# Two layers of a conditioned token mixer on one core: modulation products and half of a depthwise convolution moved from VectorE to GpSimd and ScalarE

## The chip, the core and the metric

One core of a Trainium2 chip. PE is TensorE (PEld its weight loads), DVE is VectorE, ACT is ScalarE, POOL is GpSimd, and SP issues the DMAs. The metric is the device time of one execution in microseconds, the median of a few; less is faster.

## What is computed

Two blocks of two layers each, on 512 tokens of width 1024. The change touches the first block only. Cut to that:

```python
for l in range(2):
    mod = silu(c) @ w_ada[l] + b_ada[l]          # [1, 6*1024]: "modulation"
    sh1, sc1, g1, sh2, sc2, g2 = split(mod, 6)
    h = rmsnorm(x, norm1_w[l]) * (1 + sc1) + sh1
    x = x + g1 * token_mixers(h, ...)            # convolution, attention, recurrence
    h = rmsnorm(x, norm2_w[l]) * (1 + sc2) + sh2
    x = x + g2 * conv_ffn(h, ...)
# inside token_mixers: proj = h @ w_in, split into ten parts; then
a = a_val * sigmoid(a_gate)                      # 256 channels
a = depthwise_conv(a, conv_a_w, 31 taps) + conv_a_b
a = silu(layernorm(a))
# beside it: attention over 6 heads, and a gated recurrence over 6 heads
```

The second block (sparse attention, gated linear attention, feed-forward) follows and is the same in both kernels.

## The kernel before

Activations lie with channels on the 128 partitions and the 512 tokens along the row, in fp32. A matrix product is made three times on PE from two halves of each number: a high part H (rounded to the fast fp32 type) and the rest L. So each tile of weights comes by DMA into `wraw`, ACT copies it to `wH` (line 311) and POOL subtracts to give `wL` (line 312); PE can use a tile only after both. There are 4 `wraw` and 6 `wH`/`wL` buffers.

**Modulation.** `ada` (line 520) makes one column of `mod` (128 of the 6144 numbers) at a time: a DMA of 512 KB into the tile `ada`, one DVE instruction that multiplies it with the conditioning row `c` and sums each row into `mod[:, j]` (line 528, with a small instruction that reads the accumulator), and one DVE instruction that adds the bias to this column (line 531). Columns 0 to 15 of layer 0 are made in the opening with six buffers. All others have one buffer in all, so each DMA waits for the product before it. They are a generator, `work`; `step(n)` takes n of them, and is called once for each block of projected columns in a mixer (22 times, and 3 at its end) and in a feed-forward's first half (44 times). Of layer 0 the columns 16 to 39 fall into its mixer; 44 more fall into its feed-forward; the last 12 of layer 1 fall into layer 1's mixer. Then come 50 empty steps and the table of sines for block 2.

**The mixer.** `weave` interleaves generators by their costs: each advances by cost/n, and the one that stands lowest is next. `heads(0)` and `heads(1)` (n = 93, 95) are the recurrence and then attention; `fill` (n = 100 in layer 0, 115 in layer 1) the projections and other dense products; `conv` (n = 210) the convolution. In `conv`, `conv_taps` makes the two tiles one after the other: ACT makes the first tap (line 562), and DVE the other 30 with one instruction each (line 566), y = pad * w + y. Then `conv_norm` and `conv_silu`.

The recurrence works on three pairs of heads. Each has seven levels and a crossing: ACT copies operands (line 738) of K and Q, DVE multiplies Q by a decay (line 746, `rW`) and POOL multiplies K (line 747, `rK`), PE makes 32 small products (line 706), and DVE puts them into an accumulator under a mask (line 761). The eight K products of a pair mark where the recurrence stands: they run from 77 to 125, 157 to 207 and 207 to 251 us in layer 0, and from 814 to 847, 907 to 962 and 962 to 1001 us in layer 1. Below, these are pair 0, 1 and 2.

All engines run their instructions in the order in which the scheduler of the framework wrote them, each waiting for what it needs; SP issues DMAs in such an order too.

## Time and profile before

| | |
|---|---|
| median of 3 runs (lowest, highest) | 3408.36 us (3407.62, 3408.36) |
| the profiled execution | 3403.52 us, of it the span of its instructions 3401.7 us |
| mean granted clock of TensorE | 0.983 of full speed |
| busy over the span: PE, DVE, ACT, POOL | 96%, 52%, 47%, 51% |
| layer 0: opening and mixer, feed-forward | 0 to about 410, to about 790 us |
| layer 1's mixer | about 790 to 1160 us |

Shares over the whole span say little here, since each stage has its own limits; the rows below are cut to the stages that the change touches. A clock of 1.00 is 2.4 GHz and 0.50 is 1.2 GHz, so a stretch's mean lies between.

### The profile page before, as it was taken

The numbers are of one execution on the slowest core, as the hardware profiler recorded it, in microseconds if no ns is written. First come the engines' busy times: TensorE is split into PE (matmuls) and PEld (weight loads), VectorE is DVE, ScalarE is ACT, GpSimd is POOL, SyncE is SP. The second block draws the span as 40 slices with busy tenths as digits, with TensorE's granted clock in tenths as the row PEclk, the third lists the DMA queues.
The fourth block names the chain that finished last, engine by engine and source line by source line (L and its number), as shares of the span: only waits on it lengthen the run. The fifth ranks groups of instructions, "written<-read, shape, count | busy, mean of one in ns | idle before, by whom it ended". The sixth has DMA issues, their size and how long they took to land.

```text
span 3401.7 us, 46240 instructions
## 1 busy us (share of the span) xinstructions
PE 3263.0 (96%) x16546; PEld 2655.2 (78%) x16546; DVE 1777.1 (52%) x3029; ACT 1589.6 (47%) x3104; POOL 1744.5 (51%) x1442
## 2 busy tenths in 40 slices
PE   8799999998899999999999999999999999999998
PEld 6677787787766888887878777888878787778887
DVE  8987677607976633226740735332367407353332
ACT  4457543334466544435343645443353436454433
POOL 5542366555542455553445447565634454476654
PEclk9899999999899999999999999999999999999999
DMA  6323355542212322332213132333322131322232
GB/s 231 108 71 99 115 176 178 179 132 97 87 46 68 103 99 96 99 108 86 87 57 101 52 108 81 98 97 93 102 76 87 57 101 51 108 81 98 96 94 80
DMA packets 174445, 338.92 MB, mean 100 GB/s; under 512 B 20388, under 2 KB 27428, under 8 KB 174215
## 3 DMA queue, kind: packets, MB, share of 16 engines
q1 hardware_dynamic: 174214, 335.97, 31.1%
q8 instruction: 130, 2.13, 0.3%
q14 instruction: 101, 0.82, 0.1%
HBM read 325.28 MB, written 8.91 MB: 98 GB/s over the span
## 4 chain that ended last, share of the span: by engine, by line
PE 76%; DVE 11%; issue 4%; ACT 3%; POOL 3%; DMA 2%; SPq 0%; POOLq 0%; ACTq 0%; DVEq 0%
PE p L332 22%; PE p L333 21%; PE p L334 21%; POOL wL L312 2%; DVE cv L566 2%; PE s L706 2%; DVE ada L528 1%; DMA ada<-in_w_ada 1%; PE s L1424 1%; PE s L895 1%; PE t L867 1%; PE o L625 1%; PE o L626 1%; PE s L894 1%; DVE rW L746 1%
## 5 line engine op out<-in xcount | busy, mean ns | idle before, releaser
L312 POOL TENSOR_TENSOR wL<-wraw,wH 128x512 fp32r<-128x512 f32 x996 | 1334.6, 1348 | 1278.4 <-ACT wH L311 1184.3
L332 PE MATMUL p<-hH,wH 128*128 128x512 f32 (+1 forms) x2808 | 1080.9, 386 | 12.2 <-ACT hH L311 7.5
L333 PE MATMUL p<-hL,wH 128*128 128x512 f32 (+1 forms) x2808 | 1069.5, 381 | 12.7 <-POOL hL L312 10.2
L334 PE MATMUL p<-hH,wL 128*128 128x512 f32 (+1 forms) x2808 | 1065.5, 380 | 6.2 <-POOL wL L312 6.2
L311 ACT CAST wH<-wraw 128x512 fp32r<-128x512 f32 x996 | 607.0, 613 | 947.9 <-PE p L333 436.9
L332 PEld LDWEIGHTS p<-hH,wH 128*128 128x128 f32 x2808 | 536.4, 191 | 122.4 <-issue 14.0
L333 PEld LDWEIGHTS p<-hL,wH 128*128 128x128 f32 x2808 | 537.4, 191 | 111.1 <-POOL hL L312 12.2
L334 PEld LDWEIGHTS p<-hH,wL 128*128 128x128 f32 x2808 | 536.8, 191 | 107.2 <-POOL wL L312 10.0
L1142 DVE SCALAR_TENSOR_TENSOR y<-p,vec,y 128x511 f32<-128x511 f32 (+1 forms) x264 | 196.8, 748 | 484.9 <-ACT y L1139 297.4
L332 PE MATMUL p<-aH,wH 128*128 128x512 f32 (+1 forms) x704 | 266.5, 379 | 2.9 <-ACT aH L311 2.9
L333 PE MATMUL p<-aL,wH 128*128 128x512 f32 (+1 forms) x704 | 266.5, 379 | 0.6 <-POOL aL L312 0.6
L334 PE MATMUL p<-aH,wL 128*128 128x512 f32 (+1 forms) x704 | 265.6, 377 | 0.6 <-POOL wL L312 0.6
L332 PE MATMUL p<-wH,hH 128*128 128x256 f32 x704 | 202.4, 287 | 0.0
L333 PE MATMUL p<-wL,hH 128*128 128x256 f32 x704 | 201.4, 286 | 0.0
L334 PE MATMUL p<-wH,hL 128*128 128x256 f32 x704 | 200.3, 284 | 0.0
L528 DVE SCALAR_TENSOR_TENSOR ada<-ada,c 128x1024 f32<-128x1024 f32 x96 | 144.2, 1502 | 44.3 <-DMA ada<-in_w_ada 43.6
L312 POOL TENSOR_TENSOR aL<-y,aH 128x512 fp32r<-128x512 f32 x88 | 113.9, 1295 | 98.2 <-ACT aH L311 98.2
L332 PEld LDWEIGHTS p<-aH,wH 128*128 128x128 f32 x704 | 133.2, 189 | 27.7 <-ACT aH L311 3.4
L333 PEld LDWEIGHTS p<-aL,wH 128*128 128x128 f32 x704 | 133.1, 189 | 25.8 <-POOL aL L312 1.1
L334 PEld LDWEIGHTS p<-aH,wL 128*128 128x128 f32 x704 | 133.1, 189 | 25.5 <-POOL wL L312 1.0
L706 PE MATMUL s<-rS,rS 64*128 64x128 f32 (+1 forms) x864 | 111.6, 317 | 33.9 <-DVE rW L761 21.2
L332 PEld LDWEIGHTS p<-wH,hH 128*128 128x128 f32 x704 | 135.8, 193 | 3.7 <-issue 2.9
(338 smaller groups left out, 4736.9 us busy)
## 6 DMA issues: line engine op xcount, KB each, us to landing
ada<-in_w_ada SPq DMA_DIRECT2D x96, 512.0 KB
wraw<-in_w1up SPq DMA_DIRECT2D x176, 256.0 KB
wraw<-in_w2up SPq DMA_DIRECT2D x176, 256.0 KB
wraw<-in_w2cm SPq DMA_DIRECT2D x164, 256.0 KB
wraw<-in_w1dn SPq DMA_DIRECT2D x80, 256.0 KB
wraw<-in_w2dn SPq DMA_DIRECT2D x80, 256.0 KB
wraw<-in_w1cm SPq DMA_DIRECT2D x72, 256.0 KB
wraw<-in_w2tm SPq DMA_DIRECT2D x64, 256.0 KB
```

What stands on the lines that cost most here:

```text
L311: self.nc.scalar.copy(H, src)
L312: (eng or self.nc.vector).tensor_sub(L, src, H.bitcast(F32))
L332: self.product = first = mm(out, a[0], b[0], start=start, stop=False, **kw)
L333: mm(out, a[0], b[1], start=False, stop=False, **kw)
L334: mm(out, a[1], b[0], start=False, stop=stop, **kw)
L528: ins = nc.vector.scalar_tensor_tensor(w, w, 1.0, c, op0=OP.mult, op1=OP.mult, accum_out=mod[:, j:j + 1])
L566: nc.vector.scalar_tensor_tensor(y, pad[:, j:j + S], w, y, op0=OP.mult, op1=OP.add)
L625: nc.tensor.matmul(o, v[:, i], SH[:, i], start=i == 0, stop=False)
L626: nc.tensor.matmul(o, v[:, i], SL[:, i], start=False, stop=i == n - 1)
L706: N.nc.tensor.matmul(p[:, at:at + w], K[r, ks], Q[r, qs], start=True, stop=True)
L746: nc.vector.tensor_mul(view(Q), view(Q), pattern(t, 1, (b - 1, 2), (2, m), (0, n)))
L1142: nc.vector.scalar_tensor_tensor(y[:, -d:], p[:, :S + d], c[:, i:i + 1], y[:, -d:], op0=OP.mult, op1=OP.add)
```

## The change

1. In layer 0, the columns 16 to 39 (24 of them) are made with `split`: POOL multiplies the tile by `c` in place (line 535 of the changed kernel), and ACT copies it in place with a sum of each row (line 536). All other columns stay on DVE.
2. The bias is added for a group of columns at once (`add_bias`, line 522): 15 additions in place of 96.
3. In the feed-forward, `step(2)` is called for each of the seven blocks of the second half as well: 14 columns more are made there. So layer 1's mixer holds none, and the table of sines moves from layer 1's mixer to the end of layer 0's feed-forward.
4. The convolution's two tiles are two threads of `weave`, which begin at once (n = 105 and 60, each 30 taps). Tile 0 stays on DVE. For tile 1, ACT makes each tap's product into a single buffer `ct` (line 580) and POOL adds it (line 581). `conv_norm` follows when both are done.

```diff
-CONV = (0, 210)
+CONV = (105, 60)
...
-def ada(N, l, c, mod, vec, order, pool, bufs):
+def ada(N, l, c, mod, vec, groups, pool, bufs, split=False):
...
+    for g in groups:
+        for j in range(48)[g]:
+            yield
+            w = N.tile(pool, [128, D], "ada", bufs)
+            nc.sync.dma_start(w, N.I["w_ada"][l, j])
+            if split:
+                ins = nc.gpsimd.tensor_mul(w, w, c)
+                nc.scalar.activation(w, w, AF.Copy, accum_out=mod[:, j:j + 1])
+            else:
+                ins = nc.vector.scalar_tensor_tensor(w, w, 1.0, c, op0=OP.mult, op1=OP.mult, accum_out=mod[:, j:j + 1])
...
+        add_bias(N, mod, vec, g)
...
-        nc.vector.scalar_tensor_tensor(y, pad[:, j:j + S], w, y, op0=OP.mult, op1=OP.add)
+        if i == 0:
+            nc.vector.scalar_tensor_tensor(y, pad[:, j:j + S], w, y, op0=OP.mult, op1=OP.add)
+        else:
+            t = N.tile(P, [128, S], "ct", 1)
+            nc.scalar.activation(t, pad[:, j:j + S], AF.Copy, scale=w)
+            nc.gpsimd.tensor_add(y, y, t)
...
-        weave((heads(0), HEADS), (delay(heads(1), LAG, 1), HEADS + LAG), (fill, FILL[l]), (delay(conv(), CONV[0], 1), CONV[1]))
+        weave((heads(0), HEADS), (delay(heads(1), LAG, 1), HEADS + LAG), (fill, FILL[l]), (conv(), CONV[0]), (taps(1), CONV[1]))
...
-        work = itertools.chain(ada(N, 0, c, mods[0], vecs[0], range(16, 48), B, 1),
-                               ada(N, 1, c, mods[1], vecs[1], range(48), B, 1),
+        parts = slice(0, 16), slice(16, 24), slice(24, 40), slice(40, 48)
+        work = itertools.chain(ada(N, 0, c, mods[0], vecs[0], parts[1:3], B, 1, True),
+                               ada(N, 0, c, mods[0], vecs[0], parts[3:], B, 1),
+                               ada(N, 1, c, mods[1], vecs[1], parts, B, 1),
...
-            norm.take(ct, N.dense(dn[ct], a), FULL)
+            p = N.dense(dn[ct], a)
+            step(2)
+            norm.take(ct, p, FULL)
```

**POOL in layer 0, pair 0.** From the third K product (`rK` with the decay of 4 tokens) to the fourth there stood the subtractions for two tiles of weights, two small ones for attention values (`VJ`) and another tile; the fifth K product came right behind the fourth:

```order
L747 TENSOR_TENSOR rK_601<-rK_601,rT_147_744 128x2x64x4
L312 TENSOR_TENSOR wL_992<-wraw_989,wH_991 128x512
L312 TENSOR_TENSOR wL_998<-wraw_995,wH_997 128x512
L616 TENSOR_TENSOR VJ_1112<-V_733,VJ_1112 128x4x64
L616 TENSOR_TENSOR VJ_1115<-V_733,VJ_1115 128x4x64
L312 TENSOR_TENSOR wL_1099<-wraw_1096,wH_1098 128x512
L747 TENSOR_TENSOR rK_601<-rK_601,rT_148_746 128x2x32x8
L747 TENSOR_TENSOR rK_601<-rK_601,rT_149_748 128x2x16x16
```

In the changed kernel the same stretch holds two modulation products and four additions of tile 1 (`cv_807`) as well:

```order
L762 TENSOR_TENSOR rK_593<-rK_593,rT_147_736 128x2x64x4
L535 TENSOR_TENSOR ada_761<-ada_761,c 128x1024
L581 TENSOR_TENSOR cv_807<-cv_807,ct_929 128x512
L581 TENSOR_TENSOR cv_807<-cv_807,ct_946 128x512
L312 TENSOR_TENSOR wL_994<-wraw_991,wH_993 128x512
L312 TENSOR_TENSOR wL_1000<-wraw_997,wH_999 128x512
L581 TENSOR_TENSOR cv_807<-cv_807,ct_978 128x512
L535 TENSOR_TENSOR ada_765<-ada_765,c 128x1024
L312 TENSOR_TENSOR wL_1103<-wraw_1100,wH_1102 128x512
L581 TENSOR_TENSOR cv_807<-cv_807,ct_1023 128x512
L762 TENSOR_TENSOR rK_593<-rK_593,rT_148_738 128x2x32x8
```

Over pair 0, from its first K product to its last, 5 products and 14 additions come in; between pair 0 and pair 1, 3 and 5; in pair 1, 3 and 11; to the end of pair 2, 3 more products. DVE's 30 taps of tile 0 stand ahead of the end of pair 0, all but one; before, 30 of the 60 did.

**SP at the end of layer 0's mixer.** The last three modulation columns of the group stand among the loads of `x` and of the first weights of the feed-forward (`w1up`). Before, four loads of `x` stood behind each of the last two:

```order
L527 DMA ada_3404<-in_w_ada 128x1024
L297 DMA x_3415<-in_x 128x512
L297 DMA x_3416<-in_x 128x512
L297 DMA x_3417<-in_x 128x512
L297 DMA x_3418<-in_x 128x512
L527 DMA ada_3408<-in_w_ada 128x1024
L297 DMA x_3419<-in_x 128x512
L297 DMA x_3420<-in_x 128x512
L297 DMA x_3421<-in_x 128x512
L297 DMA x_3422<-in_x 128x512
L322 DMA wraw_3580<-in_w1up 128x512
```

Now two loads are ahead of the second-last, and the last load and the weights behind the last:

```order
L297 DMA x_3469<-in_x 128x512
L297 DMA x_3470<-in_x 128x512
L533 DMA ada_3457<-in_w_ada 128x1024
L297 DMA x_3471<-in_x 128x512
L297 DMA x_3472<-in_x 128x512
L297 DMA x_3473<-in_x 128x512
L297 DMA x_3474<-in_x 128x512
L297 DMA x_3475<-in_x 128x512
L533 DMA ada_3461<-in_w_ada 128x1024
L297 DMA x_3476<-in_x 128x512
L322 DMA wraw_3634<-in_w1up 128x512
L322 DMA wraw_3640<-in_w1up 128x512
```

**DVE in layer 1, pair 1.** Here each instruction of the recurrence (`rW`, lines 746 and 761) stood between taps of tile 1 (`cv_7952`):

```order
L566 SCALAR_TENSOR_TENSOR cv_7952<-pad_7794,vec_1_77,cv_7952 128x512
L761 COPY_PREDICATED rW_8093<-sib,s_8171 128x512
L566 SCALAR_TENSOR_TENSOR cv_7952<-pad_7794,vec_1_77,cv_7952 128x512
L761 COPY_PREDICATED rW_8093<-sib,s_8172 128x512
L566 SCALAR_TENSOR_TENSOR cv_7952<-pad_7794,vec_1_77,cv_7952 128x512
L746 TENSOR_TENSOR rW_8067<-rW_8067,rT_1660_8071 128x2x64x4
L566 SCALAR_TENSOR_TENSOR cv_7952<-pad_7794,vec_1_77,cv_7952 128x512
L761 COPY_PREDICATED rW_8093<-sib,s_8214 128x512
L566 SCALAR_TENSOR_TENSOR cv_7952<-pad_7794,vec_1_77,cv_7952 128x512
L746 TENSOR_TENSOR rW_8067<-rW_8067,rT_1661_8073 128x2x32x8
L566 SCALAR_TENSOR_TENSOR cv_7952<-pad_7794,vec_1_77,cv_7952 128x512
```

Now the taps are gone from there, and the recurrence's instructions (lines 761 and 776 of the changed kernel) stand next to each other, with only the recurrence's results (`orec`) and a gate (`sg`) between:

```order
L761 TENSOR_TENSOR rW_8675<-rW_8675,rT_1822_8679 128x2x64x4
L644 TENSOR_TENSOR orec_7279<-o_8619,lo_8628 64x256
L644 TENSOR_TENSOR orec_7279<-o_8655,lo_8664 64x256
L776 COPY_PREDICATED rW_8701<-sib,s_8725 128x512
L776 COPY_PREDICATED rW_8701<-sib,s_8726 128x512
L761 TENSOR_TENSOR rW_8675<-rW_8675,rT_1823_8681 128x2x32x8
L996 SCALAR_TENSOR_TENSOR sg_8743<-p_8636,vec_1_77,sg_8743 128x512
L776 COPY_PREDICATED rW_8701<-sib,s_8777 128x512
L776 COPY_PREDICATED rW_8701<-sib,s_8778 128x512
L761 TENSOR_TENSOR rW_8675<-rW_8675,rT_1824_8683 128x2x16x16
L776 COPY_PREDICATED rW_8701<-sib,s_8810 128x512
```

Between the first K product of pair 0 in layer 1 and that of pair 1, POOL gets 15 additions; in pair 1, 11; before pair 2, 4.

## Rows read from the trace of the kernel before

**Rows 1.** Layer 0 mixer, windows: PE, PEld, DVE, ACT, POOL busy (records), clock, DMA.
```profile
77.00:125.00 48.00, 34.99 (x203) 27.73 (x203) 44.85 (x59) 18.09 (x35) 28.84 (x23) 0.82 0.34 115
125.00:157.00 32.00, 28.25 (x134) 21.25 (x133) 31.99 (x51) 15.26 (x35) 16.43 (x15) 0.95 0.32 100
157.00:207.00 50.00, 46.32 (x283) 37.40 (x282) 42.38 (x61) 29.27 (x53) 27.71 (x23) 0.90 0.20 62
207.00:251.00 44.00, 41.29 (x253) 30.77 (x251) 36.48 (x62) 27.12 (x59) 19.49 (x16) 0.96 0.22 75
251.00:360.00 109.00, 104.50 (x566) 76.95 (x566) 83.35 (x197) 78.94 (x176) 23.63 (x21) 1.00 0.27 86
360.00:400.00 40.00, 36.32 (x202) 31.52 (x201) 20.02 (x31) 16.22 (x29) 22.04 (x16) 0.96 0.58 191
```

**Rows 2.** Layer 1 mixer, windows, same columns.
```profile
814.00:847.00 33.00, 24.71 (x147) 18.94 (x146) 23.20 (x25) 15.31 (x29) 26.61 (x25) 0.90 0.36 121
847.00:907.00 60.00, 52.96 (x259) 41.08 (x261) 58.95 (x91) 25.09 (x56) 23.64 (x17) 0.89 0.28 93
907.00:962.00 55.00, 45.81 (x249) 36.07 (x246) 54.50 (x71) 26.16 (x43) 34.18 (x28) 0.89 0.17 58
962.00:1001.00 39.00, 37.25 (x235) 28.63 (x234) 28.64 (x49) 23.67 (x56) 16.47 (x16) 0.98 0.08 27
```

**Rows 3.** DVE groups, 77 to 251 us: count; busy us, mean ns; idle before.
```profile
L566 DVE SCALAR_TENSOR_TENSOR cv<-pad,vec,cv 128x512 f32<-128x512 f32 x60 | 59.0, 995 | 3.2 <-ACT cv L562 3.2
L528 DVE SCALAR_TENSOR_TENSOR ada<-ada,c 128x1024 f32<-128x1024 f32 x15 | 22.8, 1519 | 0.0
L531 DVE TENSOR_TENSOR mod<-mod,vec 128x1 f32<-128x1 f32 x15 | 5.1, 338 | 0.0
```

**Rows 4.** What PE waited for, 77 to 125 us: total us, times, longest.
```profile
PE s L706 <- DVE rW L761: 8.2, 2, 6.9
```

**Rows 5.** DVE in order of time: start, duration.
```profile
97.76 3.39 DVE L566 SCALAR_TENSOR_TENSOR cv<-pad,vec,cv 128x512 f32<-128x512 f32 x5
119.32 1.76 DVE L566 SCALAR_TENSOR_TENSOR cv<-pad,vec,cv 128x512 f32<-128x512 f32 x1
```

**Rows 6.** POOL in order of time, same moment.
```profile
118.32 2.21 POOL L312 TENSOR_TENSOR wL<-wraw,wH 128x512 fp32r<-128x512 f32 x1
```

**Rows 7.** POOL groups of the whole run by shape.
```profile
L312 POOL TENSOR_TENSOR wL<-wraw,wH 128x512 fp32r<-128x512 f32 x964 | 1312.1, 1369 | 1270.6 <-ACT wH L311 1176.7 <-PE p L334 53.4 <-DMA wraw<-in_w1open 14.9
L1512 POOL TENSOR_TENSOR y<-y,x 128x512 f32<-128x512 f32 x22 | 28.8, 1307 | 2.6 <-DVE x L1509 2.6
L1411 POOL TENSOR_TENSOR V<-V,vm 128x1024 f32<-128x1024 f32 x8 | 15.2, 1896 | 23.6 <-DVE vm L1410 14.5 <-PE p L334 8.8
```

**Rows 8.** ACT groups of the whole run by shape.
```profile
L562 ACT ACTIVATE cv<-pad,vec 128x512 f32<-128x512 f32 x4 | 3.2, 814 | 1.5 <-DVE pad L552 1.5
L1196 ACT ACTIVATE ada<-ada 128x1024 f32<-128x1024 f32 x1 | 1.1, 1061 | 0.0
```

**Rows 9.** SP issuing DMAs at the end of layer 0's mixer.
```profile
364.99 0.33 SPq L527 DMA_DIRECT2D ada<-in_w_ada  x1
370.79 0.33 SPq L527 DMA_DIRECT2D ada<-in_w_ada  x1
373.12 2.04 SPq L322 DMA_DIRECT2D wraw<-in_w1up  x4
```

**Rows 10.** Layer 0 feed-forward, windows, same columns.
```profile
577.00:660.00 83.00, 78.47 (x338) 62.70 (x338) 57.54 (x77) 30.92 (x56) 49.61 (x36) 1.00 0.55 174
680.00:775.00 95.00, 95.00 (x461) 80.38 (x460) 10.24 (x14) 27.67 (x48) 48.16 (x40) 1.00 0.42 127
```

**Rows 11.** DVE in the feed-forward, in order of time.
```profile
609.44 1.23 DVE L528 SCALAR_TENSOR_TENSOR ada<-ada,c 128x1024 f32<-128x1024 f32 x1 [1.84 <-DMA ada<-in_w_ada]
```

**Rows 12.** DVE at the start of layer 1, in order of time.
```profile
795.94 1.22 DVE L528 SCALAR_TENSOR_TENSOR ada<-ada,c 128x1024 f32<-128x1024 f32 x1
809.66 1.22 DVE L528 SCALAR_TENSOR_TENSOR ada<-ada,c 128x1024 f32<-128x1024 f32 x1
```

More of the change, by code (lines that the diff above doesn't have):

```diff
@@ L518, in silu_c, with add_bias @@
     return c
-def ada(N, l, c, mod, vec, order, pool, bufs):
+def add_bias(N, mod, vec, cols):
+    N.nc.vector.tensor_add(mod[:, cols], mod[:, cols], vec[:, cols])
+def ada(N, l, c, mod, vec, groups, pool, bufs, split=False):
     nc = N.nc
-    for j in order:
-        yield
-        w = N.tile(pool, [128, D], "ada", bufs)
-        nc.sync.dma_start(w, N.I["w_ada"][l, j])
-        ins = nc.vector.scalar_tensor_tensor(w, w, 1.0, c, op0=OP.mult, op1=OP.mult, accum_out=mod[:, j:j + 1])
-        if bufs == 1:
-            N.after(ins, N.product)
-        nc.vector.tensor_add(mod[:, j:j + 1], mod[:, j:j + 1], vec[:, j:j + 1])
+    for g in groups:
[8 more added lines that the diff above has]
+                ins = nc.vector.scalar_tensor_tensor(w, w, 1.0, c, op0=OP.mult, op1=OP.mult, accum_out=mod[:, j:j + 1])
+            if bufs == 1:
+                N.after(ins, N.product)
+        add_bias(N, mod, vec, g)
 def gated(N, mod, vec, which, name):
@@ L924, in opening @@
     ps = [N.bank(t) for t in OPEN_TAGS]
-    steps = ada(N, 0, c, mod, vec, [j for k in range(8) for j in (k, 8 + k)], P, 6)
+    steps = ada(N, 0, c, mod, vec, [slice(k, 9 + k, 8) for k in range(8)], P, 6)
     next(steps)
@@ L1012, in heads, with taps @@
                 done.add((j, e))
+        def taps(i):
+            yield from ready_when(lambda: len(pads) > i, 1)
+            yield from conv_taps(N, P, vec, pads, ys, i)
         def conv():
-            for i in range(2):
-                yield from ready_when(lambda: len(pads) > i, 1)
-                yield from conv_taps(N, P, vec, pads, ys, i)
+            yield from taps(0)
+            yield from ready_when(lambda: ys[1] is not None, 1)
             N.lnexp()
```

## The prediction

> **What bounds the kernel now.** I read the busy shares first: PE has 96% of the span, so a change on other engines pays only where PE stands still or is held at a low clock. I therefore cut both mixers along the recurrence's eight K products and looked at each stretch for the engine that is full. In layer 0, DVE is busy 44.9 of 48 us in pair 0 and 32.0 of 32 us up to pair 1, while PE has 35.0 and 28.3 us at clocks of 0.82 and 0.95. In pair 1 PE (46.3 of 50) has passed DVE (42.4), and from 207 to 360 us PE is nearly full [rows 1]. In layer 1 it is the stretch between the pairs and pair 1: DVE 59.0 of 60 and 54.5 of 55 us, PE 53.0 and 45.8 at clocks of 0.89 [rows 2]. A full DVE means that masks and decays of the recurrence queue behind taps: in pair 0 PE waits 8.2 us for the mask of line 761, once for 6.9 [rows 4]. Of DVE's time from 77 to 251 us, 60 taps took 59.0 us, 15 modulation products 22.8 and their bias 5.1 [rows 3]. So DVE's load is the real limit of four stretches, 195 us in all, of which PE leaves about 33 idle.
>
> Next, what a tap costs by itself. Five in a row took 3.39 us, 0.68 each; one took 1.76 us [rows 5]. That one stands beside POOL's subtraction, which began at 118.32, lasted 2.21 us and so ended at 120.53, while the tap ended at 121.08 [rows 6]. Each is longer than when it is alone (the tap by 1.1 us), and the mean tap of 0.995 us holds 0.3 us of this. DVE operations with two operands from SBUF and POOL's operations thus hold each other up. The SBUF — State Buffer page of the Trainium skill (SBUF: two separate sides) says that they share a port pair as an exclusive lock, held for a whole instruction, the loser blocked. The lengths in rows 5 and 6 agree with it, and taken to its end it gives the second rival below.
>
> **Prices of the new instructions.** POOL's addition of 128x512 fp32 took 1.31 us in the same form [rows 7]. The product of 128x1024 is not in the trace: it lies between 1.9 us (one operand broadcast) and two additions, 2.6 [rows 7]; I take 2.3, since both operands are full here. ACT's tap product: 0.81, its summing copy 1.06 [rows 8], and something for reading the sum. ACT is busy 18 of 48 us in pair 0 and 25 of 60 later [rows 1, 2], so 30 x 0.8 hides. The GPSIMD Engine Reference of the Trainium skill (4.1 Engine selection) puts two-operand elementwise work on GpSimd at about twice VectorE's time; 1.31 against 0.68 agrees. By it a product would be about 2 x 1.22 = 2.4, an estimate, 3 us more over 24 of them, which changes nothing.
>
> **Layer 0, pair 0.** POOL gets 5 products and 14 additions: 5 x 2.3 + 14 x 1.31 = 29.8 us on top of 28.8, so 58.6 us of work in what were 48 [rows 1, 7]. DVE loses little here, since tile 0's taps all stand there but one (30 before, 29 or so now); it loses the modulation, perhaps 5 x 1.5 [rows 3]. So POOL becomes the full engine, and the K products and weight remainders wait in its queue: behind a K product stand ACT's copy (line 738), PE's small products and the next level, and `ct`, a single buffer, makes each tap go ACT, POOL, ACT. POOL's 58.6 and some waiting give 62 us: **+14**. Low end +2 (POOL's 28.8 holds waits for DVE that may go, rows 6), high end +22 (every handover of the single buffer adds).
>
> **Up to pair 1.** POOL 16.4 + 3 x 2.3 + 5 x 1.31 = 30 us; DVE loses some 20 of the other 30 taps; PE's own 28.25 is the floor [rows 1]. 32 becomes 28: **-4** (-8 to +3). **Pair 1:** POOL 27.7 + 3 x 2.3 + 11 x 1.31 = 49 us, but part of the 27.7 was waiting for taps that are gone; PE's floor is 46.3 [rows 1]: 50 becomes 47, **-3** (-6 to +3). **Pair 2:** 3 products, 6.9 on 19.5 of 44 us; PE has 41.3 and stays the bound: 0. **251 to 360 us:** PE 104.5 of 109; a few products leave DVE (83 us busy): **-2** (-4 to 0).
>
> **The end of layer 0's mixer.** 40 us with PE busy 36.3. The last modulation loads are issued 5.8 us apart, and the feed-forward's first weights right behind [rows 9]. A load must wait until the tile before it has been read: before by one DVE product of about 1.2, now by POOL's 2.3 and then ACT's 1.1, so each round is about 2.2 longer, and SP's loads of `x` and `w1up` stand behind. Two to three rounds: **+5** (0 to +9). Layer 0 together: 14 - 4 - 3 - 2 + 5 = **+10**.
>
> **Layer 0's feed-forward.** In the first half nothing changes: two modulation products per block, each waiting for its DMA [rows 11]. The second half gets 14 more; DVE is busy 10 of 95 us there and PE 95 of 95 [rows 10], so 14 x 1.23 = 17 us hide. What could show is the loads: 14 x 0.5 MB in 95 us on top of 127 GB/s comes to about 204, where the first half moves 174 with PE at 78.5 of 83 [rows 10]. But a round of 5.8 us twice is less than a block (95 / 7 = 13.6). **0** (0 to +4). The bias in groups saves 81 instructions of a third of a microsecond [rows 3], counted in the stretches; the opening waits for its DMAs, **0**. The sine table moves under the same idle DVE, **0**.
>
> **Layer 1.** Ahead of pair 0 stood modulation products [rows 12], three before 814 us and two in the pair; with them and their bias gone the stretch to 847 us and its approach gain about **-5** (-8 to 0; PE has only 24.7 of 33 us of work there, but POOL is at 26.6 [rows 2]). To pair 1: by the order of instructions DVE loses 39 - 25 = 14 taps and, of the twelve columns, I put five here: 14 x 1.0 + 5 x 1.5 = 21.5 of its 59 us [rows 2, 3]; POOL gets 15 additions, 23.6 + 19.7 = 43. PE's 53.0 at a clock of 0.89 would be 47 at full clock; so 60 becomes 52: **-8** (-13 to 0). Pair 1: DVE loses 20 taps and the last two columns, 23 us, from 54.5 to about 31; POOL 34.2 + 11 x 1.31 = 48.6, less its waits; PE 45.8 x 0.89 = 41 as floor [rows 2]. 55 becomes 46: **-9** (-14 to 0). Pair 2: 4 additions, 5 us on 16.5 of 39; PE at 37.3 stays: 0. Together **-22**.
>
> **Sum.** +10 - 22 = -12 us. The profiled execution took 3403.5 us, the median of the runs is 3408.4, 0.14% above; -12 makes 3391.5 for a profile and 3396 for the median. I predict 3396.
>
> **Rivals.** First, *layer 0 gains too* (POOL absorbs all). POOL idles 19 us in pair 0 and half of the next stretches [rows 1], and PE's waits for DVE were real [rows 4]. With the low ends, +2 - 8 - 6 - 4 + 0 = -16, and layer 1's -22: -38, 3370 us. Against it: 58.6 us of POOL do not fit in 50.
>
> Second, *the work is only put on a slower engine behind the same door* (slower). If a DVE operation with two operands and a POOL operation never overlap [rows 5, 6], then what counts is the sum of both. In layer 0 up to 251 us POOL gets 29.8 + 13.5 + 21.3 + 6.9 = 71.5 us and DVE gives up 30 x 0.68 + 15 x 1.22 = 38.7: +33. In layer 1, 30 x 1.31 = 39.3 against 30 x 0.68 + 12 x 1.22 = 35: +4. All of it on the path gives +37, 3445 us; half, 3427. It decides once POOL is without a gap through pairs 0 and 1 of layer 0, 108 us instead of 98. Against it: in layer 1 and pair 1 PE has idle time that can take it, and masks need not wait for taps. This is where the rule of the SBUF — State Buffer page (SBUF: two separate sides) would lead.
>
> Third, *no net change*: pair 0 at its high end (+22) with the rest of layer 0 as forecast costs 18, a weaker layer 1 (-17) pays for it; about 3408.
>
> **How the numbers follow.** The forecast (layer 0 at +4 to +16, layer 1 at -16 to -30) has 0.42; it alone spans 3382 to 3408, nearly all of it faster. Layer 0 gains: 0.22. Slower by the shared door: 0.19. No net change: 0.17. For 8 in 10 I cut below the first rival and at the half price of the second: 3366 to 3427. A measurement of this kernel tells about 0.2%, 6.8 us, from no change. Faster by more than that: 0.22 and 0.37 of the forecast, 0.59; same: 0.05 and 0.16, 0.21; slower: 0.19 and 0.01, 0.20.
>
> **What would show it.** Right: in layer 0 the K products of pair 0 span about 62 us with POOL above 90% and PE's longest waits naming POOL's K product or `ct`; in layer 1 the stretch from the first K product of pair 0 to the last of pair 1 takes 126 to 131 us instead of 148, with DVE under 70% and a higher clock. Taps of tile 0 in pair 0 should stay near 1 us. The second half of the feed-forward keeps PE full. Wrong: POOL's additions well above 1.31 us, or DVE's taps above 1.2, speak for the shared door; a pair 0 at or below 50 us for the first rival. A round of modulation much longer than 8 us would put the loss at the end of layer 0's mixer, where `w1up` then arrives late and PE stands; and if PE loses several microseconds in the feed-forward's second half, the loads were not hidden.

## The result, and the profile after

The changed kernel takes 3441.53 us (median of 4, 3435.71 to 3444.51), against 3407.99 for the kernel before (median of 4): a ratio of 1.0100, 95% interval [1.0082, 1.0117], so 33.5 us slower. The forecast was 3396, the range ended at 3427. The profiled executions, one of each kernel, lie 40.7 us apart by their spans (3442.4 and 3401.7). All stretches below are read from such single executions, and all totals are medians of runs.

The stages first. These are windows of the changed kernel: PE, PEld, DVE, ACT, POOL busy (records), granted clock, share of the DMA engines, GB/s. The first line is pair 0 of layer 0, from its first K product to its last; then the way to pair 1, pair 1, pair 2, and the rest of the mixer in two parts. They answer to [rows 1].

```profile
81.00:143.00 62.00, 33.40 (x158) 25.52 (x158) 56.87 (x42) 30.85 (x57) 60.50 (x36) 0.72 0.23 77
143.00:170.60 27.60, 19.69 (x97) 15.10 (x98) 17.43 (x23) 17.74 (x40) 26.03 (x21) 0.75 0.27 92
170.60:218.00 47.40, 37.65 (x226) 30.25 (x225) 23.40 (x30) 27.44 (x53) 41.82 (x35) 0.87 0.18 63
228.00:277.00 49.00, 45.77 (x247) 32.55 (x244) 30.20 (x46) 35.37 (x67) 28.89 (x21) 0.97 0.21 70
277.00:400.00 123.00, 112.67 (x593) 81.91 (x592) 80.14 (x183) 87.68 (x192) 43.02 (x30) 0.97 0.25 84
400.00:445.00 45.00, 37.37 (x200) 32.00 (x199) 17.25 (x26) 20.00 (x38) 26.74 (x19) 0.92 0.54 176
```

Layer 1 in the same view: pair 0, the way to pair 1, pair 1 up to pair 2, pair 2 (they answer to [rows 2]). Then two windows of layer 0's feed-forward, in its first and second half (to [rows 10]).

```profile
851.00:884.00 33.00, 27.31 (x176) 21.76 (x176) 15.97 (x18) 15.43 (x29) 25.61 (x26) 0.90 0.21 73
884.00:947.00 63.00, 46.95 (x231) 35.26 (x230) 47.15 (x68) 31.95 (x67) 40.08 (x30) 0.89 0.13 42
947.00:996.00 49.00, 39.48 (x247) 32.01 (x245) 31.06 (x37) 29.90 (x58) 45.22 (x42) 0.83 0.10 33
996.00:1037.00 41.00, 38.17 (x252) 29.94 (x252) 21.07 (x37) 20.70 (x47) 22.96 (x19) 1.00 0.17 53
...
618.00:701.00 83.00, 78.56 (x339) 62.69 (x338) 50.32 (x64) 31.89 (x59) 50.48 (x36) 1.00 0.55 178
721.00:816.00 95.00, 95.00 (x462) 80.47 (x461) 39.53 (x51) 28.49 (x49) 50.92 (x41) 1.00 0.59 191
```

In pair 0 POOL is busy 60.5 of 62 us, and PE's clock is at 0.72. Cut at the start of the K products and of the load of the feed-forward's first weights, the 40.7 us are made up as follows (us, with the prediction's terms beside them):

| stretch | before | after | difference | forecast |
|---|---|---|---|---|
| start to first K product | 77.4 | 80.9 | +3.5 | 0 |
| pair 0 and the way to pair 1 | 79.5 | 89.7 | +10.2 | +10 |
| pair 1 and the way to pair 2 | 56.2 | 57.4 | +1.2 | -3 |
| pair 2 | 36.6 | 48.7 | +12.1 | 0 |
| to the feed-forward's first weights | 123.4 | 138.7 | +15.3 | +3 |
| to layer 1's first K product | 441.0 | 435.9 | -5.1 | up to -5 |
| layer 1, first to last K product | 185.5 | 185.1 | -0.4 | -17 to -22 |
| rest | 2402.1 | 2406.0 | +3.9 | 0 |

Pair 2's first K product starts at 213.1 us in layer 0 of the kernel before, and at 968.4 in layer 1; the 207 and 962 that are given above for it are the ends of pair 1.

A single row of the table can be work that was moved. So here are both layers cut once more, first before and then after: layer 0 from pair 0's first K product to pair 2's first, and on to pair 2's last; layer 1 from pair 0's first K product to pair 1's last, and on to pair 2's last.

```profile
77.42:213.08 135.66, 114.96 (x656) 90.36 (x654) 124.99 (x176) 67.00 (x133) 74.03 (x61) 0.89 0.28 92
213.08:249.72 36.64, 34.19 (x196) 25.19 (x196) 29.26 (x53) 22.53 (x49) 16.97 (x13) 0.95 0.21 72
814.14:960.85 146.71, 122.19 (x646) 95.12 (x645) 135.50 (x184) 65.51 (x127) 83.14 (x68) 0.89 0.26 87
960.85:999.61 38.76, 37.01 (x231) 28.36 (x231) 28.39 (x49) 23.46 (x57) 16.46 (x16) 0.96 0.07 22
...
80.88:227.99 147.11, 100.84 (x571) 80.34 (x572) 102.67 (x104) 82.48 (x168) 132.26 (x95) 0.79 0.22 74
227.99:276.73 48.74, 45.51 (x246) 32.39 (x245) 29.93 (x46) 35.11 (x67) 28.63 (x20) 0.97 0.21 71
851.28:981.74 130.46, 101.23 (x555) 77.57 (x553) 82.42 (x105) 66.61 (x129) 97.59 (x82) 0.87 0.14 49
981.74:1036.44 54.70, 49.84 (x346) 40.65 (x343) 32.00 (x51) 30.92 (x72) 35.44 (x32) 0.97 0.14 44
```

In layer 1 the stretch to the end of pair 1 is 16.3 us shorter, close to the -17 (-8 and -9) of the forecast, and what follows is 15.9 us longer: PE has 346 instructions there in place of 231, and 49.8 us of work in place of 37.0. In layer 0, 11.3 us of PE's work have come into pair 2. Over layer 0's three pairs together PE was busy about as long as before (146 us against 149), and their length rose by 23.5. So the loss is time in which PE stands, and beside it the clock up to pair 2 is lower (0.79 against 0.89). The table's last row, 2406.0 us, lies within what this stretch takes in the kernels below (2399.5 to 2406.3), so nothing is read from it.

Next, whom the engines waited for, from 80 to 277 us of the changed kernel (us in total, times, longest):

```profile
ACT ct L580 <- POOL cv L581: 28.1, 18, 3.5
...
ACT ada L536 <- POOL ada L535: 24.5, 12, 4.2
...
PE s L721 <- ACT rW L743: 17.1, 2, 15.5
PE s L721 <- DVE rW L776: 15.0, 5, 5.0
```

The first two lines are new. ACT, of which the prediction said that its work hides, stood 52.6 us (28.1 and 24.5) before its new instructions because POOL had not finished its part, and 7.7 us more from 277 to 415 us. PE's longest wait, 15.5 us, is for a copy of ACT; before, it was 6.9 for DVE [rows 4].

The instructions themselves, in pair 0 (81 to 143 us), DVE's taps of tile 0 and POOL's groups: count, busy us, mean ns:

```profile
L577 DVE SCALAR_TENSOR_TENSOR cv<-pad,vec,cv 128x512 f32<-128x512 f32 x25 | 44.2, 1768 | 0.6
...
L581 POOL TENSOR_TENSOR cv<-cv,ct 128x512 f32<-128x512 f32 x14 | 22.2, 1586 | 1.4 <-ACT ct L580 1.4
L312 POOL TENSOR_TENSOR wL<-wraw,wH 128x512 fp32r<-128x512 f32 x8 | 13.6, 1705 | 0.1
L535 POOL TENSOR_TENSOR ada<-ada,c 128x1024 f32<-128x1024 f32 x5 | 13.6, 2719 | 0.0
```

And one moment of it in order of time, four taps on DVE and what POOL ran beside them:

```profile
103.81 7.75 DVE L577 SCALAR_TENSOR_TENSOR cv<-pad,vec,cv 128x512 f32<-128x512 f32 x4
...
103.18 3.42 POOL L312 TENSOR_TENSOR wL<-wraw,wH 128x512 fp32r<-128x512 f32 x2
106.56 1.71 POOL L581 TENSOR_TENSOR cv<-cv,ct 128x512 f32<-128x512 f32 x1
108.22 2.79 POOL L535 TENSOR_TENSOR ada<-ada,c 128x1024 f32<-128x1024 f32 x1
```

Four taps took 7.75 us where they take 2.7 alone [rows 5]: in step with four instructions of POOL, which ran from 103.18 to 111.01 us. The mean tap rose from 0.995 us [rows 3] to 1.77.

### The profile page after: what moved, and what is told of

Its sections match the earlier page's. It is cut to its first block, busy times and chain, and to the rows that moved or that the text cites. A ratio compares the mean times of both kernels' runs of the same rounds, so it can differ in the third digit from the quotient of the medians.

```text
span 3442.4 us, 46273 instructions
## 1 busy us (share of the span) xinstructions
PE 3262.2 (95%) x16546; PEld 2653.4 (77%) x16546; DVE 1704.9 (50%) x2840; ACT 1645.2 (48%) x3209; POOL 1871.9 (54%) x1526
## 4 chain that ended last, share of the span: by engine, by line
PE 75%; DVE 8%; POOL 7%; ACT 4%; issue 3%; DMA 2%; SPq 0%; POOLq 0%; ACTq 0%; DVEq 0%
PE p L332 22%; PE p L333 21%; PE p L334 21%; POOL wL L312 2%; POOL cv L581 2%; DMA ada<-in_w_ada 1%; PE s L910 1%; PE s L1446 1%; PE t L882 1%; PE s L721 1%; POOL ada L535 1%; PE o L640 1%; DVE ada L538 1%; PE o L641 1%; POOL rK L762 1%
## 5 line engine op out<-in xcount | busy, mean ns | idle before, releaser
L333 PE MATMUL p<-hL,wH 128*128 128x512 f32 (+1 forms) x2808 | 1067.1, 380 | 11.9 <-POOL hL L312 9.5
L332 PEld LDWEIGHTS p<-hH,wH 128*128 128x128 f32 x2808 | 537.1, 192 | 123.6 <-issue 14.2
L538 DVE SCALAR_TENSOR_TENSOR ada<-ada,c 128x1024 f32<-128x1024 f32 x72 | 122.4, 1700 | 95.7 <-DMA ada<-in_w_ada 95.7
L721 PE MATMUL s<-rS,rS 64*128 64x128 f32 (+1 forms) x864 | 104.8, 331 | 68.1 <-DVE rW L776 24.7
L721 PEld LDWEIGHTS s<-rS,rS 64*128 64x128 f32 x864 | 80.1, 214 | 96.4 <-ACT rW L743 25.7
```

The lines of the kernel that those rows point to most:

```text
L332: self.product = first = mm(out, a[0], b[0], start=start, stop=False, **kw)
L333: mm(out, a[0], b[1], start=False, stop=False, **kw)
L538: ins = nc.vector.scalar_tensor_tensor(w, w, 1.0, c, op0=OP.mult, op1=OP.mult, accum_out=mod[:, j:j + 1])
L721: N.nc.tensor.matmul(p[:, at:at + w], K[r, ks], Q[r, qs], start=True, stop=True)
```

## The experiments

Differences below are to the kernel before in the runs of the same chip (medians 3404.2 to 3406.5). "Neither" is the changed kernel with both splits undone. "Layer 0's pairs" are the time from pair 0's first K product to pair 2's last, and "the rest of the mixer" is the time from there to the load of the feed-forward's first weights.

**The change in its parts.** Four kernels: the modulation split without the convolution's, the reverse, neither, and the convolution split in layer 1 alone. Where a layer's convolution is back on DVE, its two tiles again stand in one thread of `weave` (n = 210; this part of the edit is not shown).

```diff
# neither; the other three keep one of the two edits, or the second by layer
-        if i == 0:
+        if i == 0 or dve:
...
-ada(N, 0, c, mods[0], vecs[0], parts[1:3], B, 1, True),
+ada(N, 0, c, mods[0], vecs[0], parts[1:3], B, 1),
```

> Only the grouped bias and the 14 columns in the feed-forward's second half remain; modulation of layer 0 and both tiles are on DVE. Both theories: layer 0's mixer as before within 3 us, layer 1 about 5 us shorter than before, the second half of the feed-forward no longer: 3398 to 3406.

Measured 3394.0, -12.5 (ratio 0.9964, [0.9951, 0.9976]), a little more gain than forecast.

> The modulation of layer 0 is split as in the changed kernel, the convolution is back on DVE in both layers. Theory D (shared door: DVE operations with two operands and POOL operations exclude each other, and POOL is without a gap in layer 0): pair 0 gets 5 products of 2.7 us, 28.8 + 13.6 = 42 of 48 us, so POOL still has gaps; pair 0 near 52 us, the end of pair 2 some 8 us later than before, and the end of the mixer 12 us more; in all +15 to +20 us over the kernel before, less 5 in layer 1. Theory H (handovers: each round of a single buffer goes through POOL, ACT and a DMA, and ACT stands in its queue): the same end of the mixer, and nothing in the pairs: +8.

Measured 3430.8, +24.3 (1.0070, [1.0055, 1.0085]): 36.8 over neither, more than either theory gave. Layer 0's pairs took 189.6 us against 170.2 with neither, the rest of the mixer 139.4 against 125.2.

> The convolution's tile 1 is on ACT and POOL as in the changed kernel, the modulation of layer 0 is back on DVE. Theory D: POOL gets 14 additions of 1.59 us in pair 0, 51 us of work, and DVE keeps 5 products more: pair 0 near 56 us with taps of about 1.5 us on DVE; the end of pair 2 about +12, nothing more at the mixer's end, layer 1 as in the changed kernel: +8 to +14 in all. Theory H: the single product buffer makes 30 rounds of ACT and POOL, 2.05 us each, and the pairs are as long as in the changed kernel: +20 at the end of pair 2.

Measured 3426.6, +20.1 (1.0052, [1.0035, 1.0070]); its four runs scatter from 3416 to 3431, and the profiled one is the fastest. Layer 0's pairs took 185.1 us against 170.2 with neither, the rest of the mixer 126.7 against 125.2: hardly anything is lost there. Pair 2 ended 12 us later than before (261.8 us against 249.7), as theory D had it, but the median is above its range, and this profile can't show where the other 10 us lie.

> As the kernel with neither, but layer 1's tile 1 on ACT and POOL. Theory D: layer 1's POOL has room (40 of 63 and 45 of 49 us busy in the changed kernel), so about as fast as the kernel with neither, 0 to -5 against it. Theory H: the handovers hold up pair 2, +5 to +10 against it.

Measured 3400.9, -5.6 (0.9987, [0.9977, 0.9996]), so 6.9 slower than neither, within what theory H gave: where the forecast had put its main gain, there is a loss. Layer 1's pairs took 187.8 us against 180.3.

Of the rest, the bias alone. The opening's 16 columns keep an addition each, so this kernel has 73 additions fewer, where the change has 81 fewer:

```diff
-        nc.vector.tensor_add(mod[:, j:j + 1], mod[:, j:j + 1], vec[:, j:j + 1])
+        if groups is None:
+            nc.vector.tensor_add(mod[:, j:j + 1], mod[:, j:j + 1], vec[:, j:j + 1])
+        for g in groups or ():
+            if g.stop == j + 1:
+                nc.vector.tensor_add(mod[:, g], mod[:, g], vec[:, g])
```

> The kernel before with the bias added by groups, nothing else. Of the 12.5 us that the kernel with neither split gains, either the bias is the larger part, since each small addition takes 0.34 to 1.2 us of a full DVE: 3396 to 3401; or the 14 columns in the feed-forward's second half are: 3403 to 3408.

Measured 3399.5, -4.9 (0.9983, [0.9973, 0.9993]). So the grouped bias is worth about 5 us. That lies in the range which the forecast had for "the larger part", and yet is the smaller part of 12.5: about 7.6 are left, by subtraction and not by a run, for the 14 columns in the feed-forward's idle half and for the rest of the grouping. The two splits cost 36.8 and 32.6 us over neither alone and 46 together, so their costs overlap; no run shows where.

**The shared door.** In the changed kernel, 29 of 30 taps of tile 0 are left out in layer 0:

```diff
+        if i == 0 and skip and j > 1:
+            continue
```

> The changed kernel, with 29 of the 30 taps of tile 0 left out in layer 0, so that DVE has hardly an operation with two operands to set against POOL's additions and products, which stay as they are. Theory D (shared door): in pair 0 POOL's additions fall from 1.59 us to about 1.28 and the weight remainders from 1.66 to about 1.3, POOL's work from 61 to about 51 us, and pair 0 from 62 to 51 to 54 us; the end of pair 2 some 15 us earlier, 3420 to 3428 in all. Theory Q (POOL's own amount of work and its handovers set the pace, DVE's taps do not matter): pair 0 stays above 58 us, 3434 to 3441.

Measured 3432.0, +27.8 (1.0080, [1.0062, 1.0098]): between the two. POOL's groups from 79 to 134 us, where pair 0 lies now:

```profile
L583 POOL TENSOR_TENSOR cv<-cv,ct 128x512 f32<-128x512 f32 x14 | 18.7, 1337 | 2.5 <-ACT ct L582 2.3
L535 POOL TENSOR_TENSOR ada<-ada,c 128x1024 f32<-128x1024 f32 x5 | 12.3, 2455 | 0.0
L312 POOL TENSOR_TENSOR wL<-wraw,wH 128x512 fp32r<-128x512 f32 x9 | 11.5, 1292 | 1.0 <-ACT wH L311 1.0
```

The additions and weight remainders have about the lengths that theory D gave (1.34 and 1.29 us), the products took 2.46, and pair 0 takes 54.1 us. But the three pairs still take 187.0 us, 14.7 more than in the kernel before, which has all of DVE's taps. Leaving out the taps gave back 9 us of layer 0's pairs (5.7 us by the medians), and in this the door and DVE's own time for the taps lie together; so the door alone is not the bulk. The next two, with 58 of 60 taps left out, ask the same of the modulation split alone.

> Neither edit, with the same 58 taps of layer 0 left out: the base for the run before. DVE loses some 58 us of work in layer 0, of which PE's idle time in the pairs and its low clock can give back 20 to 30: 3364 to 3376. What counts is the difference to the run before: 22 or less by theory D, 30 or more by theory Q.

> The modulation split alone, with 58 of the 60 taps of layer 0 left out; it is to be read beside the kernel with neither edit and the same taps left out. With all taps the modulation split costs 36.8 us (3430.8 - 3394.0). Theory D (the door: POOL's products make DVE's taps longer, 1.45 us against 1.00, and DVE is still full in pair 0): without taps the cost falls by the 15 to 20 us of the pairs, to 22 or less. Theory Q (POOL's own work and the rounds through POOL and ACT): it stays at 30 or more.

Measured 3374.1 (-31.4; 0.9909, [0.9893, 0.9926]) and 3413.9 (+8.4; 1.0025, [1.0014, 1.0036]). The modulation split costs 39.8 us without taps, 36.8 with them: by the bounds that were set, theory D falls for it, though POOL's products were shorter without taps (a median of 2.39 us against 2.59). In the second kernel ACT waited 47.4 us for POOL's products from 80 us to the end of the mixer. This pair does not price the door with the taps in place, since without taps DVE is no longer full (layer 0's pairs took 145.3 us without the split).

**Rounds and queues.** If not the door, then what? The last four columns on DVE again, in the kernel with the modulation split alone:

```diff
-parts[1:3], B, 1, True)
-parts[3:], B, 1)
+(parts[1], slice(24, 36)), B, 1, True)
+(slice(36, 40), parts[3]), B, 1)
```

> The modulation split alone (both tiles of the convolution on DVE), but its last four columns, which are made at the end of layer 0's mixer, on DVE again. If the 16 us lost between the end of pair 2 and the feed-forward's first weights are the longer rounds of the single modulation buffer, they go: 139 us there become 124 to 127, 3415 to 3419 in all against 3431. If they come from POOL's and ACT's queues being late already, or from the clock, no more than 4 us go: 3427 to 3431.

Measured 3426.9, +22.7 (1.0062, [1.0043, 1.0080]), 1.6 less than without the edit, which is not clear of the scatter (3418.6 to 3430.1), and 136.0 us after pair 2 in place of 139.4. So the longer round at the mixer's end, the forecast's +5, is at most 3.4 us and not where the 15 come from. This is what ACT did there in the kernel with the modulation split alone, in order of time (start, duration):

```profile
278.62 0.50 ACT L311 CAST W<-rW 128x128 fp32r<-128x128 f32 x2
282.22 1.06 ACT L536 ACTIVATE ada<-ada 128x1024 f32<-128x1024 f32 x1 [3.11 <-POOL ada L535]
283.18 0.19 ACT L536 ACTIVATION_READ_ACCUMULATOR ada<-ada 128x1 f32 x1
283.28 0.88 ACT L311 CAST W<-rW 128x128 fp32r<-128x128 f32 x4
```

and what POOL did meanwhile:

```profile
276.77 1.27 POOL L312 TENSOR_TENSOR wL<-wraw,wH 128x512 fp32r<-128x512 f32 x1 [1.57 <-ACT wH L311]
279.81 2.38 POOL L535 TENSOR_TENSOR ada<-ada,c 128x1024 f32<-128x1024 f32 x1 [1.77 <-DMA ada<-in_w_ada]
```

ACT has made two of the six casts of `W`. The sum stands next in its queue. POOL's product waits for its load until 279.81 and ends at 282.19, and so ACT does nothing for 3.1 us while the other four casts lie behind the sum. They ran from 283.28 on, and behind them further copies, for the last of which PE stood 4.8 us until 286.18. The wait table of that kernel, from 80 to 410 us, has 15 such stands:

```profile
ACT ada L536 <- POOL ada L535: 47.3, 15, 6.5
```

A sum that is issued a step later, with other work of ACT ahead of it:

```diff
-                ins = nc.gpsimd.tensor_mul(w, w, c)
-                nc.scalar.activation(w, w, AF.Copy, accum_out=mod[:, j:j + 1])
+                N.after(nc.gpsimd.tensor_mul(w, w, c), N.product)
+                late = j < 39
+                if late:
+                    yield
+                ins = nc.scalar.activation(w, w, AF.Copy, accum_out=mod[:, j:j + 1])
```

> The modulation split alone, and ACT's summing copy of a column is issued a step later, behind other work of ACT, so that ACT's queue does not stand for POOL's product. Theory A (the loss after pair 2, 139 us there against 125 with neither, comes from ACT standing in its queue before the sum, 9.7 us, while the attention's copies of W are behind it): 139 becomes 128 to 132 and the total 3420 to 3424. Rival (POOL's own load and the clock): less than 4 us, 3427 to 3431.

Measured 3425.0, +19.5 (1.0064, [1.0049, 1.0079]), 4.8 better by medians, and 136.7 us after pair 2; its profiled execution is the slowest of the four and no shorter than that of the kernel without the edit. The wait wasn't removed but spread: the buffer is held longer, so POOL now stands 30.5 us for the load, against 5.3 without the edit (from 80 to 402 us).

```profile
POOL ada L537 <- DMA ada<-in_w_ada: 30.5, 10, 8.0
ACT ada L541 <- POOL ada L537: 29.4, 8, 7.1
```

So the wait was taken away altogether: ACT sums parts of `c`, which it need not wait for (`after` keeps the order in the queues and makes no wait).

```diff
-                nc.scalar.activation(w, w, AF.Copy, accum_out=mod[:, j:j + 1])
+                z = N.tile(pool, [128, 128], "adz", 1)
+                for k in range(3):
+                    N.after(nc.scalar.activation(z, c[:, 128 * k:128 * k + 128], AF.Copy, accum_out=mod[:, j:j + 1]), ins)
```

> The modulation split alone, but ACT sums parts of c itself (three copies of 128x128 for each column, about as long together as the sum) in place of POOL's product, so it never waits for POOL; the modulation's values are left out by this. POOL's products stay. Theory A (ACT, which runs in order, stands before the sum until POOL has come to the product: 47.3 us, 15 times, between the first K product and the end of the mixer with the modulation split, and copies for the recurrence and the attention stand behind it): most of the 37 us go, 3397 to 3409. Theory Q (POOL's load of 24 products holds up its K products and weight remainders): 3420 to 3431.

Measured 3409.8, +5.5 (1.0017, [1.0008, 1.0027]): half of the cost is gone, 18.0 over neither in place of 36.8. Its two windows, the pairs and the rest of the mixer:

```profile
81.00:262.30 181.30, 141.42 (x844) 107.26 (x846) 148.07 (x182) 101.78 (x268) 127.93 (x85) 0.89 0.24 80
262.30:389.70 127.40, 121.56 (x632) 91.85 (x631) 86.43 (x189) 91.85 (x235) 48.12 (x35) 0.96 0.30 96
```

The same two of the kernel with the modulation split alone:

```profile
80.50:270.10 189.60, 153.33 (x823) 116.51 (x823) 148.30 (x179) 101.59 (x207) 122.56 (x83) 0.81 0.22 75
270.10:409.50 139.40, 125.87 (x652) 93.39 (x651) 84.22 (x191) 94.95 (x206) 52.23 (x35) 0.96 0.28 92
```

The rest of the mixer is back at 127.4 us with POOL as busy as before: its loss was ACT's standing (or the part of the buffer's round that ACT held, which this edit takes away with it). In the pairs 8 of 19 us went. There PE's longest wait for the copy `rW` of ACT fell from 12.3 to 6.8 us, but another for DVE's mask `rW` came up, 14.6 us where 5.7 was the longest. For the other part, POOL's product is left out:

```diff
-                ins = nc.gpsimd.tensor_mul(w, w, c)
-                nc.scalar.activation(w, w, AF.Copy, accum_out=mod[:, j:j + 1])
+                ins = nc.scalar.activation(w, w, AF.Copy, accum_out=mod[:, j:j + 1])
```

> The modulation split alone, with POOL's product left out: ACT sums the loaded tile. Theories A and Q both let the cost fall, to 3396 to 3406; if it stays above 3420, it is ACT's sum itself (24 x 1.25 us) or its wait for the load that costs.

Measured 3396.2, -8.1 (0.9977, [0.9968, 0.9986]), 4.4 over neither. So, in this order of taking away, 18.8 of the 36.8 us went with ACT's standing (and the longer hold of the buffer), 13.6 with POOL's products, and 4.4 are left with ACT's sums, less what DVE gained by making 24 products fewer. Another order could divide them otherwise.

**The convolution.** In both layers POOL adds the shifted input in place of ACT's product, so that no engine waits for the other.

```diff
-            nc.scalar.activation(t, pad[:, j:j + S], AF.Copy, scale=w)
-            nc.gpsimd.tensor_add(y, y, t)
+            a = nc.scalar.activation(t, pad[:, j:j + S], AF.Copy, scale=w)
+            if j > 1:
+                N.after(a, last)
+            last = nc.gpsimd.tensor_add(y, y, pad[:, j:j + S])
+            N.after(last, a)
```

> The convolution split alone in both layers, but POOL adds the shifted input in place of ACT's product, which ACT still makes: the scaling of tile 1's taps is left out, and neither engine waits for the other. The instructions of both engines and their number stay. Theory A (ACT stands in its queue for the single product buffer: 42.8 us in layer 0's pairs, 28 in layer 1's): layer 0's pairs 185 to about 173 us, layer 1's 185 to 178, 3400 to 3410 in all. Theory Q (POOL's load of 30 additions for each tile, and the door): 3418 to 3428.

Measured 3415.7, +11.4 (1.0031, [1.0018, 1.0044]): 8.7 better by medians, but the runs of the two kernels overlap, and its span of 3413.6 is about that of the split kernel's profile (3414.7). Layer 0's pairs stayed long, 187.3 us against 185.1, though ACT's 42.8 us of standing were gone. In pair 0, 64.0 us long, POOL was busy 62.9 us and DVE 59.6; PE's longest wait there was 11.9 us for DVE's mask, where it had been 14.2 for ACT's copy. So in layer 0 the standing is not what makes the pairs long; POOL's 30 additions beside 30 taps on DVE are left for it. Layer 1's pairs went from 185.2 to 178.4, below neither's 180.3 (with 148.1 us of PE's work in them where neither has 158.6, so part of it is work that moved on). The way to pair 1 stayed at 64.0 us (63.4 with the wait); pair 1 with the way to pair 2 fell from 49.3 to 41.6. Layer 1 apart, with two buffers for the product:

```diff
-            t = N.tile(P, [128, S], "ct", 1)
+            t = N.tile(P, [128, S], "ct", 1) if j % 2 else N.tile(P, [128, S], "tmp", N.ntmp)
```

> The convolution split in layer 1 alone, with two buffers for a tap's product (every second one from the ring of tmp tiles) in place of one. Theory H (the loss of 7 us against the kernel with neither is the round ACT, POOL, ACT of a single buffer, in which ACT's queue stands): layer 1's pairs, 187.8 us from the first to the last K product with one buffer and 180.3 with neither, take 180 to 182, 3394 in all. Theory D: they stay at 185 or more, 3399 to 3402.

Measured 3406.2, +2.0 (1.0002, [0.9992, 1.0011]); the pairs take 187.8 us as with one buffer, and theory H's 180 to 182 failed. The way to pair 1 did shorten, from 63.9 to 56.8 us, but pair 1 with the way to pair 2 took 54.4 in place of 49.3 and pair 2 took 44.8 in place of 42.9. ACT's waits for POOL's addition fell only from 28.0 to 19.1 us. The ring of `tmp` tiles serves the recurrence as well, so this run is not a second buffer alone.

> The convolution split in layer 1 alone, with 29 of the 30 taps of tile 0 left out there. Theory D: POOL's additions run at about 1.26 us and layer 1's pairs shorten by 7 us or more, from 187.8 to 181 or less, 3394 or less in all. Theory H: the 30 rounds of the product buffer stay, and the pairs stay at 185 or more, 3399 to 3402.

Measured 3394.3, -10.0 (0.9969, [0.9956, 0.9982]), the pairs 174.7 us. This lies in theory D's range, but the additions take 1.32 us against 1.38, so what the missing taps gave is mostly DVE's time: the second pad is made 8 us earlier (853.3 us in place of 861.6), since it stood behind taps in DVE's queue, and the additions begin with it. The whole gain in the pairs lies on the way to pair 1 (53.0 us in place of 63.9) and in pair 2 (40.5 in place of 42.9); pair 1 with the way to pair 2 stays at 49.3.

Last, ten taps of tile 1 in place of 30 for ACT and POOL (`dve` is set for layer 0):

```diff
-        if i == 0 or dve:
+        if i == 0 or dve or j % 3:
```

> The convolution split in layer 1 alone, and there only 10 of tile 1's 30 taps (every third) on ACT and POOL, the others on DVE. Theory P (the additions that stand ahead of pair 1 in the queues of ACT and POOL, one round of over 2 us after the other, hold up its first operands): a third of them hold up little, and DVE is lighter by 10 taps; layer 1's pairs 175 to 180 us, 3388 to 3394 in all. Rival (DVE's taps and POOL's additions in one chain through the same tile and the same door): 3396 to 3402.

Measured 3394.4, -11.2 (0.9969, [0.9958, 0.9980]): the pairs take 176.7 us, and ten additions in place of 30 undo the loss, although DVE has 20 taps more than with 30 additions. They gain nothing clear over neither.

So the version that beats both kernels is neither, with no split: 0.9964 of the kernel before, about 1.3% below the changed one.

## Why the prediction was wrong, point by point

**What was right.** Pair 0 of layer 0 with the way to pair 1 came out at +10.2 against +10, with POOL gapless (60.5 of 62 us) where the sum had 58.6. This number is in part luck: the additions and products took 35.8 us where 29.8 was forecast, since they run longer beside the taps, and POOL's other work took 24.7 in place of 28.8. The product took 2.40 us in a free moment and 2.72 in pair 0, against 2.3. The second half of the feed-forward took 14 columns more and kept PE at 95.0 of 95 us.

**The step that failed** is the sentence "ACT is busy 18 of 48 us in pair 0 and 25 of 60 later [rows 1, 2], so 30 x 0.8 hides". It took busy time for the cost. Each new instruction of ACT needs POOL's (the sum after the product, the next `ct` after the addition), ACT runs its queue in order (the casts at 283.28 us above), and behind it lie the copies of K, Q and `W` and the weights' high parts. It stood 52.6 us up to the end of layer 0's pair 2 and 7.7 after that. With the modulation alone, taking that standing away gave back 18.8 of 36.8 us, 12 of them in the rest of the mixer, where the forecast had +3 and the table has +15.3. There the forecast named another mechanism, the buffer's round at the very end; the run with the last four columns on DVE leaves 3.4 us to it at most. For the convolution in layer 0 the same step is not shown to have cost anything: there the pairs stayed long without the standing.

**"Pair 2: 0"** is the other step that failed, in both layers (+12.1 in layer 0; in layer 1 +9.3, and +6.6 on the way to it). The forecast took PE's work in each stretch as fixed and let a gain ahead of pair 2 stand. But PE's instructions moved. In layer 1, which was to gain 22 us, the time from pair 0's first K product to pair 1's last came to 130.5 us, inside the 126 to 131 that were named as the sign of being right, and DVE was busy 82.4 us of it, under 70% as named; only the clock was not higher (0.87 against 0.89). Then PE's work behind pair 1 grew by 12.8 us, and the layer's pairs ended 0.4 us shorter. Inside the stretch the terms were wrong as well: the way to pair 1 did not fall by 8 but rose by 1.3 (61.9 to 63.2), and pair 1 fell by 18.9 (54.0 to 35.1), not by 9. The forecast's 14 and 20 taps are more than the 30 that left DVE; in the trace they are 10 and 20.

The loss of layer 1 against neither (185.2 us against 180.3 in the pairs) goes with tile 1's chain of 30 rounds of ACT and POOL: 178.4 without its wait, and 176.7 with ten rounds, though that one has more taps on DVE. What holds up the way to pair 1 is not settled. It shortens with two buffers or without tile 0's taps, but not without the wait; DVE's taps there took a mean of 1.14 us without the wait against 1.02 in the changed kernel.

**The first 81 us** (+3.5, forecast 0): a product and its sum stand ahead of pair 0 (the product at 69.0 us), and the forecast priced neither. All kernels with POOL's products start pair 0 at 79.6 to 81.0 us, those with the modulation on DVE at 76.7 to 77.5.

**The second rival** (3445, or 3427 at half) is the case that came nearest, and its condition held in pair 0 (POOL 60.5 of 62 us), though not in pair 1 (41.8 of 47.4). The signs named for it came as well: additions of 1.59 us and taps of 1.77 in pair 0. That 3441.5 lies so near its 3445 is luck: its mechanism was only a part, and the 33.5 us are 46 lost less 12.5 gained by parts of the change that it did not price apart. The SBUF — State Buffer page of the Trainium skill (SBUF: two separate sides) says that the loser of the shared port blocks for a whole instruction; the four taps in 7.75 us agree. But with the taps left out, the modulation split costs as much as with them, and the changed kernel's pairs shorten by 9 us of 23.5.

**The by-products** were not priced apart: the forecast counted the bias and the 14 columns inside its stretches. They gave 12.5 us by themselves, about 5 of it the grouped bias. What the two splits then cost over that, 46 us, is more than the 33.5 of the result shows.

What stays open is how layer 0's loss from the convolution (some 26 us by medians, 16 in the profile) divides between POOL's additions and the door, since no run took the additions away and left the taps in place with the rest unchanged. Open too is how much of the cost is the lower clock.

## What to carry to other kernels

An operation that is divided over two engines costs, besides its time on each, the time for which the second one stands in its queue until the first has finished its part. What that costs is set by the work that lies behind it in the queue, not by how idle the engine was. Before moving work to an engine with free time, look in the wait table for what it would have to wait for and how late that engine runs; here a later issue gave back 4.8 of 36.8 us and a further buffer nothing, since the producer stayed as late. When a stretch gets shorter, look whether its work left or only moved into the next one. And try the small by-products of a change by themselves: here they were the whole gain.

## What the runs showed of the hardware

DVE and POOL slowed each other: when POOL had no gap (pair 0), DVE's mean tap went from 0.995 us to 1.77, and POOL's addition from 1.34 (taps left out) to 1.59, so both were longer, not only one. In the moment shown above, four taps and four POOL instructions went side by side, as if they took turns by whole instructions. PE's granted clock was lower where PE stood more: 0.72 in pair 0 with PE busy 33.4 of 62 us, against 0.82 with 35.0 of 48 before [rows 1].
